# Split f32r projections for five more xbc tiles, a held SSD decay and a new stage order in a one-core S5/SSD/retention trunk

## Chip, cores and metric

The kernel runs on 1 core of one Trainium2 chip. The metric is device time in microseconds, the median of the runs. The engines are named as in the profile: PE or TensorE (matmuls), ACT (ScalarE), DVE (VectorE), POOL (GpSimd) and SP (SyncE, which issues all DMAs here).

## What is computed

Input x is (1, 512, 1024) in float32; the trunk has two layers and a final RMSNorm. Layer 0, in which the change lies, is this, cut to what matters:

```python
p = rmsnorm(h) @ w_in                     # 1024 -> z 2048 | S5 input 1024 | xBC 1536 | dt 16
y_a = s5_mixer(p[S5 input], ...) * silu(z[:1024])
xbc = silu(causal_depthwise_conv(p[xBC], conv_w, conv_b))     # 4 taps
dt  = softplus(p[dt] + dt_bias)
a_cs = cumsum(dt * a)                                         # in chunks of 128 steps
y_diag = (C B^T * exp(segsum(a_cs))) @ (xs * dt)              # decay matrix per head
states, y_off = chunk states, C @ previous state * exp(a_cs)
y_b = rmsnorm((y_diag + y_off + xs * D) * silu(z[1024:]), groups=2)
h = h + concat([y_a, y_b]) @ w_out
```

S5 is a diagonal complex recurrence; its gated output passes a GLU. Layer 1 is a four-head retention layer, untouched by the change.

## The kernel before

All activations lie transposed, features on the 128 partitions and the 512 steps along the free axis, so 1024 features are 8 tiles x0 to x7. Each output tile of 128 columns of the input projection is one "projection": 8 matmuls over the 8 input tiles into one PSUM bank (tag acc, 3 banks).

There are two forms of a projection (`proj`, L214). Plain (`mm1`, L210): 8 float32 matmuls of the raw weight with the normed input xn. Split (`mm3`, L111): weight and input are each the sum of a part rounded to f32r and a remainder, and 24 f32r matmuls make high x high, high x low and low x high. The weight is split after its load by `split_w` (L101): ACT rounds it (L107), DVE subtracts (L108), both with the rank of `rank_w`. Names in the list `SPLIT` (L29) take the split form. The input's parts xh and xl are made by stage `w` (`parts`, L259, through `split`, L119). The 16 parts and xn0 to xn6 share the 16 buffers of tag "x", so seven parts take over a buffer of xn and wait until all plain projections that are traced before have read it. Plain weights use seven buffers (tags raw, wh, wl in turn); split ones have three raw buffers and two each for the two parts.

The work of layer 0 is cut into stages, which `ORDER` (L36) lists by letter and number: d and e make dt and its cumulative sums (e also writes a_cs to DRAM), x is a projection of xBC with its convolution (`conv`, L345), u one of the S5 input, z one of the gate (written to DRAM, L432), s an SSD chunk's setup (`ssd`, L359) and t its output (`ssd_y`, L409), w the input's parts, n and r the SSD norm (root and use), o a tile of the output projection's SSD half (`out_b`), p a tile of the S5 gate (`glu_in`). S5 has q (parameters and the rotation table on POOL), l, g, a (load, state products and scan of a group), b and k (kernel and taps), c (its output).

A scheduler turns this into one queue for each engine: it runs a list of instructions against a simulated timeline and, of those that are ready, takes the one with the lowest priority number, which by default counts up in the order of tracing. `rank_w` gives weight splits -2000000 and `rank_e` (L92) gives evacuations of PSUM -1000000, plus a count. A queue is then fixed, and each engine takes its instructions in that order.

Stage x: ACT evacuates the bank with the last tap and the bias (L349), DVE adds the other three taps from PSUM (L352, rank_e), ACT applies SiLU (L354). The bank is free after the last tap. Stage s transposes the chunk's x into PSUM (tag b, 3 banks); DVE evacuates it twice, with dt (xdt, L380) and with the decay to the chunk's end (xds, L384); PE makes the chunk's state (L387) and the part of the previous state (L390), which DVE evacuates into yos (L392); DVE moves the running state on (L406, L407). For the decay matrix, a_cs is loaded as a broadcast (512 KB, L395), ACT takes 8 absolute differences (L397) and one exponential (L398), DVE multiplies by C B^T (L399).

At the start, u0 and u1 are projected from the scaled, not yet normed x (L247, L249). The squares are added on DVE (L243), `root` (L162) sums them over partitions with matmuls into rs0ps and takes the inverse square root in small DVE steps (L150 to L159), `spread` (L172) transposes it into rs0pb, ACT copies it (L176), and DVE makes xn (L251).

Of the kernel before, what the change touches and what calls it, by code (L numbers as in the profile page):

```python
# [14 lines left out]
AF = mybir.ActivationFunctionType  # L15
ALU = mybir.AluOpType
# [9 lines left out]
BUFS = {'x': 16, 'v': 17, 'm': 20, 's': 4, 'p': 5, 'f': 8}  # L26
POOL_P = ((1, 1), (2, 1), (3, 1))
WARM = 11
SPLIT = [f"z{m}" for m in range(16)] + [f"u{m}" for m in range(2, 8)]  # L29
SILU_Z = tuple(range(8, 16))  # L30
GELU_P = ()
AX, AZ = 200, 600
KEEP = (2, 3)
POOL_Z = (7,)
VEC_X = ((0, 0), (1, 0), (0, 1), (1, 1))
ORDER = """d0 x8 x10 x9 e0 x11 q0 x0 b0 x1 x2 l0 g0 x3 x4 k0 x5 b1 x6 a0 x7 w0 g1 s0 u2 u3 l1 t0 s1 z0 a1 k1 b2 z1 t1 s2 u4 c0 u5  # L36
 t2 l2 g2 s3 z2 a2 k2 b3 z3 t3 u6 c1 u7 z4 l3 g3 z5 n0 z6 a3 z7 c2 n1 z8 k3 r0 z9 r1 z10 c3 z11 o0 p0 p1 o1 z12 p2 z13 p3 o2 z14
 p4 p5 z15 o3 p6 p7 o4 o5 o6 o7"""
MAGIC = 12582912.0
LOG2E = 1.4426950408889634  # L40
LN2_HI = 0.693359375
# [7 lines left out]
def trunk_kernel(ctx: ExitStack, tc: tile.TileContext, a: dict, out: bass.AP):  # L49
# [98 lines left out]
    def rsqrt_small(y, ss, n, name, w=4):  # L148
# [6 lines left out]
        for it in range(3):  # L155
# [3 lines left out]
            vec.scalar_tensor_tensor(y, t, 1.5, cur, op0=ALU.add, op1=ALU.mult)  # L159
            cur = y  # L160

    def root(sqs, n, name):  # L162
        ps = aux(name + "ps")
        for c in range(NC4):
            for i, s in enumerate(sqs):
                pe.matmul(ps[:, c:c + 1], s[:, c * P:(c + 1) * P], ones,
                          start=i == 0, stop=i == len(sqs) - 1)
        y = sm.tile([P, 4], F32, name=name + "y", tag="rs_y", bufs=4)
        rsqrt_small(y, ps[:, 0:4], n, name)
        return y  # L170

    def spread(y, name, bc):  # L172
        pb = aux(name + "pb")
        for c in range(NC4):
            pe.transpose(pb[:, c * P:(c + 1) * P], y[:, c:c + 1].broadcast_to([P, P]), ident)
        act.activation(bc, pb, AF.Copy)  # L176

    def rstd(sqs, n, name, bc):
        y = root(sqs, n, name)
        spread(y, name, bc)  # L180
        return y
# [12 lines left out]
    def layer0():  # L194
# [33 lines left out]
        with rank(-3000000):  # L228
            s5pr = t("m", "s5p", n=192).rearrange("p (i w) -> p i w", w=64)
            sp.dma_start(s5pr, a["s5p"])  # L230
            sp.dma_start(lnw, a["lnw"])
            w0 = []
            for k in range(KD):
                sp.dma_start(xs[k], a["xT"][k])
                if k == 0:
                    w0 += [ld_raw(a["w_u"][m], f"u{m}") for m in range(1)]
            w0 += [ld_raw(a["w_u"][m], f"u{m}") for m in range(1, 2)]
            for k in range(KD):
                q = t("p", f"xq{k}")
                act.activation(q, xs[k], AF.Square)  # L240
                act.activation(xs[k], xs[k], AF.Identity, scale=lnw[:, 0, k:k + 1])
                if k:
                    vec.tensor_tensor(sq[0], sq[0], q, op=ALU.add)  # L243
                sq.append(q)
            pu = [acc(f"u{m}") for m in range(2)]
            for k in range(KD):
                pe.matmul(pu[0], w0[0][:, k, :], xs[k], start=k == 0, stop=k == KD - 1)  # L247
            rstd(sq[:1], D, "rs0", rbc)
            mm1(pu[1], w0[1], xs)  # L249
            for k in range(KD):  # L250
                vec.tensor_tensor(xn[k], xs[k], rbc, op=ALU.mult)  # L251
        tri = const("tri", [P, P], a["tri"])
# [88 lines left out]
            sp.dma_start(at_d.rearrange("c h l -> h c l"), aT)  # L341

        xbc = [None] * 12

        def conv(m):  # L345
            ps = proj(a["w_xbc"][m], f"xbc{m}", ahead=AX)
            g = t("v", f"cva{m}")
            with rank_e():
                act.activation(g, ps, AF.Identity, scale=cvw[:, m, 3:4], bias=cvw[:, m, 4:5])  # L349
                for j in range(2, -1, -1):  # L350
                    d = 3 - j
                    vec.scalar_tensor_tensor(g[:, d:], ps[:, 0:SEQ - d], cvw[:, m, j:j + 1], g[:, d:],  # L352
                                             op0=ALU.mult, op1=ALU.add)
            act.activation(g, g, AF.Silu)  # L354
            xbc[m] = g
        prev = [None, None]
        held = {}

        def ssd(c):  # L359
            yb, bT, cT = xbc[0:8], xbc[8:10], xbc[10:12]  # L360
# [13 lines left out]
            for gr in range(2):  # L374
                hs = slice(8 * gr, 8 * gr + 8)
                xdt = t("v", f"xdt{c}{gr}").rearrange("p (h d) -> p h d", d=64)
                ps_x = aux(f"px{c}{gr}", "b")
                for i in range(4):
                    pe.transpose(ps_x[:, i * P:(i + 1) * P], xbc[4 * gr + i][:, cs], ident)
                vec.tensor_tensor(xdt, ps_x.rearrange("p (h d) -> p h d", d=64),  # L380
                                  dtn[:, c, hs].unsqueeze(2).broadcast_to([P, 8, 64]), op=ALU.mult)
                if c < NC4 - 1:
                    xds = t("v", f"xds{c}{gr}")
                    vec.tensor_tensor(xds.rearrange("p (h d) -> p h d", d=64), ps_x.rearrange("p (h d) -> p h d", d=64),  # L384
                                      ds[:, c, hs].unsqueeze(2).broadcast_to([P, 8, 64]), op=ALU.mult)
                    ps_s = aux(f"st{c}{gr}", "b")
                    pe.matmul(ps_s, bn[:, gr, :], xds, start=True, stop=True)  # L387
                if c > 0:
                    ps_o = aux(f"yo{c}{gr}", "b")
                    pe.matmul(ps_o, cT[gr][:, cs], prev[gr], start=True, stop=True)  # L390
                    yo = t("v", f"yos{c}{gr}")
                    vec.tensor_tensor(yo.rearrange("p (h d) -> p h d", d=64), ps_o.rearrange("p (h d) -> p h d", d=64),  # L392
                                      ec[:, c, hs].unsqueeze(2).broadcast_to([P, 8, 64]), op=ALU.mult)
                dec = tp.tile([P, 8, P], F32, name=f"dec{c}{gr}", tag="g", bufs=3)
                sp.dma_start(dec, at_d[c, hs, :].partition_broadcast(P))  # L395
                for i in range(8):
                    act.activation(dec[:, i, :], dec[:, i, :], AF.Abs, bias=nacs[:, c, 8 * gr + i:8 * gr + i + 1])  # L397
                act.activation(dec, dec, AF.Exp, scale=-1.0)  # L398
                vec.tensor_tensor(dec, dec, cbm[:, gr, :].unsqueeze(1).broadcast_to([P, 8, P]), op=ALU.mult)  # L399
                held[c, gr] = xdt, dec, yo if c > 0 else None  # L400
                if c == 0:
                    prev[gr] = t("s", f"prev{gr}")
                    act.activation(prev[gr], ps_s, AF.Copy)
                elif c < NC4 - 1:
                    h_ = prev[gr].rearrange("p (h d) -> p h d", d=64)
                    vec.tensor_tensor(h_, h_, cd[:, c, hs].unsqueeze(2).broadcast_to([P, 8, 64]), op=ALU.mult)  # L406
                    vec.tensor_tensor(prev[gr], prev[gr], ps_s, op=ALU.add)  # L407

        def ssd_y(c):  # L409
            yb, cs = xbc[0:8], slice(c * P, (c + 1) * P)  # L410
# [731 lines left out]
```

## Time and profile before

| what | value |
|---|---|
| three runs | 917.1, 919.69 (median), 923.75 us |
| the profiled execution | 923.73 us |
| its span, first to last instruction | 921.9 us |
| mean granted clock of TensorE | 0.970 |
| busy: PE, DVE, ACT, POOL | 881.6, 524.6, 360.3, 212.7 us |

The profile shows one execution. Times in rows are microseconds from the span's start unless marked ns; a name such as xbc4w is a tile of the program, L212 a line of the code. A busy PE is not PE at its peak, since the ends of matmuls are modelled. "Granted clock" is the share of TensorE's full clock that the chip let it have in a stretch; 1.00 is 2.4 GHz.

### The profile page before, as it was taken

What the parts mean: (1) busy time and instruction counts of PE and PEld (TensorE: products, weight loads), DVE (VectorE), ACT (ScalarE), POOL (GpSimd) and SP (SyncE); (2) the same over time, 40 slices, a digit from 0 to 9 for tenths busy, and PEclk for the clock granted to TensorE, in tenths of its full rate; (3) what the DMA queues carried; (4) which work ended last, traced back from release to release, by engine and by line L of the source; (5) the groups of instructions that cost most, each with busy time, mean ns of one, the idle gap of its engine ahead of it and who ended that gap; (6) DMA issues with size and microseconds to landing.
All of it is one profiled execution on the core that took longest, in us unless ns stands there. A gap on an engine that the chain in (4) does not pass through costs nothing.

```text
span 921.9 us, 11425 instructions
## 1 busy us (share of the span) xinstructions
PE 881.6 (96%) x4308; PEld 678.6 (74%) x4308; DVE 524.6 (57%) x917; ACT 360.3 (39%) x571; POOL 212.7 (23%) x187
## 2 busy tenths in 40 slices
PE   8899797989989999999999999999999999999996
PEld 4244355757768877788888888888888888888885
DVE  6967469784873365443454463744743644547445
ACT  4344632515216444523344225345421244254432
POOL 0059983070472500000003121301000303110020
PEclk9999899979999888999999999999999999999999
DMA  7377142666549636573543222222222221222322
GB/s 242 113 211 249 50 128 69 187 201 180 146 130 311 216 132 190 182 245 125 202 141 103 92 91 69 74 86 69 92 92 94 93 90 66 92 69 69 114 69 92
DMA packets 64184, 121.45 MB, mean 132 GB/s; under 512 B 18112, under 2 KB 28672, under 8 KB 64000
## 3 DMA queue, kind: packets, MB, share of 16 engines
q1 hardware_dynamic: 64128, 120.71, 40.7%
q8 instruction: 34, 0.56, 0.3%
q14 instruction: 22, 0.18, 0.1%
HBM read 103.61 MB, written 17.07 MB: 131 GB/s over the span
## 4 chain that ended last, share of the span: by engine, by line
PE 76%; DVE 11%; issue 4%; ACT 4%; DMA 2%; POOL 1%; SPq 0%; DVEq 0%; POOLq 0%; ACTq 0%
PE xbc L212 3%; PE qk L117 3%; PE g L115 3%; PE qk L116 3%; PE g L116 3%; PE g L117 3%; PE qk L115 3%; PE v L921 3%; PE v L922 3%; PE v L920 3%; PE z L117 2%; PE z L115 2%; PE z L116 2%; PE ob L116 2%; PE ob L117 2%
## 5 line engine op out<-in xcount | busy, mean ns | idle before, releaser
L894 POOL TENSOR_TENSOR rt<-rt,ru 128x512 f32<-128x512 f32 x16 | 27.2, 1721 | 134.6 <-DVE ru L893 134.6
L963 POOL TENSOR_TENSOR os<-os,os 128x512 f32<-128x512 f32 x12 | 15.5, 1290 | 139.8 <-ACT os L961 106.9
L352 DVE SCALAR_TENSOR_TENSOR cva<-xbc,cvw,cva 128x511 f32<-128x511 f32 (+2 forms) x36 | 26.8, 743 | 25.8 <-ACT cva L349 25.4
L789 POOL TENSOR_TENSOR O<-ct,s5pws 128x512 f32<-128x512 f32 x16 | 23.1, 1441 | 50.0 <-DVE prev L407 42.0
L873 POOL TENSOR_TENSOR hs<-hs,hs 128x512 f32<-128x512 f32 x7 | 12.2, 1749 | 92.4 <-ACT hs L871 92.4
L397 ACT ACTIVATE dec<-dec,nacs 128x128 f32<-128x128 f32 x64 | 19.4, 389 | 33.6 <-DMA dec<-at_d 33.6
L893 DVE TENSOR_TENSOR ru<-qk,tab 128x512 f32<-128x512 f32 x16 | 10.9, 684 | 32.5 <-PE qk L117 32.5
L793 POOL TENSOR_TENSOR O<-O,ot 128x512 f32<-128x512 f32 x16 | 24.6, 1563 | 0.0
L452 POOL TENSOR_TENSOR za6r<-za6r,y 128x512 f32<-128x512 f32 x1 | 2.2, 2247 | 86.3 <-DMA h_d<-hb 86.3
L789 POOL TENSOR_TENSOR ot<-ct,s5pws 128x512 f32<-128x512 f32 x16 | 21.7, 1355 | 0.0
L733 POOL TENSOR_TENSOR tm<-al,b 128x512 f32<-128x512 f32 x6 | 8.1, 1371 | 55.6 <-DMA b<-in_s5bP_dram 32.9
L995 DVE TENSOR_TENSOR h<-h,out 128x512 f32<-128x512 f32 x8 | 5.5, 686 | 25.5 <-PE out L117 25.5
L1056 POOL TENSOR_TENSOR fin<-fin,fnw 128x512 f32<-128x512 f32 x4 | 5.0, 1289 | 59.5 <-ACT fq L1020 59.5
L836 PE MATMUL Y<-T,U 128*64 128x128 f32 x128 | 18.4, 311 | 0.0
L526 POOL TENSOR_TENSOR s5rt<-rot,s5lv 128x512 f32<-128x512 f32 (+4 forms) x7 | 5.9, 837 | 52.8 <-DVE s5lv L668 52.8
L490 DVE TENSOR_TENSOR hb<-ob,hb 128x512 f32<-128x512 f32 x8 | 5.5, 690 | 20.9 <-PE ob L117 20.8
L416 PE MATMUL y<-ident,yos 128*128 128x128 f32 x48 | 12.6, 349 | 4.6 <-DVE yos L392 4.6
L839 ACT ACTIVATE ysb<-Y 128x256 f32<-128x256 f32 x16 | 5.2, 380 | 29.9 <-PE Y L836 18.8
L733 DVE TENSOR_TENSOR tm<-al,b 128x512 f32<-128x512 f32 x10 | 11.3, 1168 | 9.9 <-DMA b<-in_s5bP_dram 6.8
L519 DVE TENSOR_TENSOR h<-oa,h 128x512 f32<-128x512 f32 x8 | 5.5, 691 | 19.6 <-PE oa L117 19.6
L835 PE MATMUL Y<-Or,X 128*64 128x128 f32 x64 | 14.5, 314 | 1.5 <-DMA Or<-o_d 1.5
L120 ACT ACTIVATE rh<-rt 128x512 fp32r<-128x512 f32 (+1 forms) x16 | 9.1, 577 | 16.9 <-POOL rt L894 16.9
(1697 smaller groups left out, 2972.3 us busy)
## 6 DMA issues: line engine op xcount, KB each, us to landing
al<-al_d SPq DMA_DIRECT2D x8, 512.0 KB
b<-in_s5bP_dram SPq DMA_DIRECT2D x8, 512.0 KB
dec<-at_d SPq DMA_DIRECT2D x8, 512.0 KB
o_d<-O SPq DMA_DIRECT2D x16, 256.0 KB
T<-kd SPq DMA_DIRECT2D x64, 64.0 KB
Or<-o_d SPq DMA_DIRECT2D x16, 256.0 KB
x<-in_xT_dram SPq DMA_DIRECT2D x8, 256.0 KB
u_d<-us SPq DMA_DIRECT2D x8, 256.0 KB
```

The source lines that it names most:

```text
L115: pe.matmul(ps, wh[:, k, :], xh[k], start=start and i == 0, stop=False)
L116: pe.matmul(ps, wh[:, k, :], xl[k], start=False, stop=False)
L117: pe.matmul(ps, wl[:, k, :], xh[k], start=False, stop=stop and i == len(ks) - 1)
L212: pe.matmul(ps, raw[:, k, :], x[k], start=k == 0, stop=k == KD - 1)
L352: vec.scalar_tensor_tensor(g[:, d:], ps[:, 0:SEQ - d], cvw[:, m, j:j + 1], g[:, d:], op0=ALU.mult, op1=ALU.add)
L397: act.activation(dec[:, i, :], dec[:, i, :], AF.Abs, bias=nacs[:, c, 8 * gr + i:8 * gr + i + 1])
L789: pool.tensor_tensor(x.rearrange("p (g k c) -> p g k c", g=4, c=16), ct[:, c, par, 4 * hf:4 * hf + 4].unsqueeze(2).broadcast_to(sh), pws[: ...
L793: pool.tensor_tensor(o, o, tm, op=ALU.add)
L894: pool.tensor_tensor(t1, t1, t2, op=op)
L920: pe.matmul(ps[c], hh[kk][:, cs], wh[:, i, :], start=kk == 0, stop=False)
L921: pe.matmul(ps[c], hh[kk][:, cs], wl[:, i, :], start=False, stop=False)
L922: pe.matmul(ps[c], hl[kk][:, cs], wh[:, i, :], start=False, stop=kk == KD - 1)
```

## The change

Five xbc projections (m = 3 to 7) take the split form. Stage w stands behind x2 instead of behind x7, and x3 to x6 follow each other. A few z tiles, the glu_in and the out_b tiles change places. At the start u1's matmuls are queued on PE behind the root's. ACT's absolute differences of the decay are queued behind the last evacuation of a conv stage that was traced before them, which is xbc7's for all chunks. Six DVE steps of the SSD setup get the rank of evacuations.

```diff
-SPLIT = [f"z{m}" for m in range(16)] + [f"u{m}" for m in range(2, 8)]
+SPLIT = [f"z{m}" for m in range(16)] + [f"u{m}" for m in range(2, 8)] + [f"xbc{m}" for m in range(3, 8)]
...
-ORDER = """d0 x8 x10 x9 e0 x11 q0 x0 b0 x1 x2 l0 g0 x3 x4 k0 x5 b1 x6 a0 x7 w0 g1 s0 u2 u3 l1 t0 s1 z0 a1 k1 b2 z1 t1 s2 u4 c0 u5
- t2 l2 g2 s3 z2 a2 k2 b3 z3 t3 u6 c1 u7 z4 l3 g3 z5 n0 z6 a3 z7 c2 n1 z8 k3 r0 z9 r1 z10 c3 z11 o0 p0 p1 o1 z12 p2 z13 p3 o2 z14
- p4 p5 z15 o3 p6 p7 o4 o5 o6 o7"""
+ORDER = """d0 x8 x10 x9 e0 x11 q0 x0 b0 x1 x2 w0 l0 g0 x3 x4 x5 x6 k0 b1 a0 x7 g1 s0 u2 u3 l1 t0 s1 z0 a1 z1 k1 b2 t1 s2 u4 c0 u5
+ t2 l2 g2 s3 z2 a2 z3 k2 b3 t3 u6 c1 u7 z4 l3 g3 z5 n0 z6 a3 z7 c2 n1 z8 k3 r0 z9 z10 r1 c3 z11 p0 p1 z12 p2 z13 p3 o0 o1 z14
+ p4 p5 o2 z15 p6 p7 o3 o4 o5 o6 o7"""
...
+    held0 = [None]
+
     def root(sqs, n, name):
...
-                pe.matmul(ps[:, c:c + 1], s[:, c * P:(c + 1) * P], ones,
-                          start=i == 0, stop=i == len(sqs) - 1)
+                held0[0] = pe.matmul(ps[:, c:c + 1], s[:, c * P:(c + 1) * P], ones,
+                                     start=i == 0, stop=i == len(sqs) - 1).ins
...
-            rstd(sq[:1], D, "rs0", rbc)
-            mm1(pu[1], w0[1], xs)
+            y0, last = root(sq[:1], D, "rs0"), held0[0]
+            with tc.issue_after(last):
+                mm1(pu[1], w0[1], xs)
+            spread(y0, "rs0", rbc)
...
-                act.activation(g, ps, AF.Identity, scale=cvw[:, m, 3:4], bias=cvw[:, m, 4:5])
+                held["conv"] = act.activation(g, ps, AF.Identity, scale=cvw[:, m, 3:4], bias=cvw[:, m, 4:5]).ins
...
-                vec.tensor_tensor(xdt, ps_x.rearrange("p (h d) -> p h d", d=64),
-                                  dtn[:, c, hs].unsqueeze(2).broadcast_to([P, 8, 64]), op=ALU.mult)
+                with rank_e():
+                    vec.tensor_tensor(xdt, ps_x.rearrange("p (h d) -> p h d", d=64),
+                                      dtn[:, c, hs].unsqueeze(2).broadcast_to([P, 8, 64]), op=ALU.mult)
...
-                for i in range(8):
-                    act.activation(dec[:, i, :], dec[:, i, :], AF.Abs, bias=nacs[:, c, 8 * gr + i:8 * gr + i + 1])
+                with tc.issue_after(held["conv"]):
+                    for i in range(8):
+                        act.activation(dec[:, i, :], dec[:, i, :], AF.Abs, bias=nacs[:, c, 8 * gr + i:8 * gr + i + 1])
```

The steps of xds, yos and the running state (two) are put under rank_e in the same way as xdt. `issue_after(ins)` puts an edge of order, without a semaphore, from `ins` to each instruction in the block on the same engine.

## Rows read from the trace of the kernel before

**Rows 1.** Page, part 2: TensorE's busy tenths and granted clock, 40 slices.
```profile
PE   8899797989989999999999999999999999999996
...
PEclk9999899979999888999999999999999999999999
```

**Rows 2.** TensorE's waits, 20 to 440 us: us in total, times, longest.
```profile
PE xbc L212 <- issue: 6.2, 2, 5.1
PE y L416 <- DVE yos L392: 4.6, 1, 4.6
PE u L117 <- DVE u3l L108: 3.7, 1, 3.7
...
PE ob L115 <- ACT ybh L120: 2.2, 1, 2.2
```

**Rows 3.** Windows: length, busy PE, PEld, DVE, ACT, POOL, PEclk, DMA share, GB/s.
```profile
86.00:126.00 40.00, 34.94 (x111) 15.35 (x110) 13.92 (x22) 22.53 (x39) 38.45 (x44) 0.91 0.24 92
126.00:198.00 72.00, 62.53 (x405) 46.07 (x403) 65.77 (x87) 23.18 (x43) 27.00 (x18) 0.96 0.50 152
...
198.00:210.00 12.00, 12.00 (x80) 8.50 (x80) 5.53 (x13) 4.70 (x14) 7.10 (x6) 0.55 0.59 199
335.00:350.00 15.00, 12.46 (x85) 10.35 (x84) 8.80 (x24) 7.72 (x12) 0.00 (x0) 0.61 0.41 124
```

**Rows 4.** Timeline of TensorE, 80 to 137: start, length, instruction [idle before, releaser].
```profile
81.27 7.11 PE L212 MATMUL xbc<-xn,xbc2w 128*128 128x512 f32 x16 [1.11 <-issue]
88.21 7.03 PE L212 MATMUL xbc<-xn,xbc3w 128*128 128x512 f32 x16
...
100.64 9.93 PE L212 MATMUL xbc<-xn,xbc4w 128*128 128x512 f32 x16 [5.06 <-issue]
...
136.14 0.61 PE L364 MATMUL cb<-cva,cva 128*128 128x128 f32 x4
```

**Rows 5.** Timeline of TensorE, first matmuls of two split projections.
```profile
179.78 0.50 PE L115 MATMUL u<-xh,u4h 128*128 128x512 f32 x1
...
185.36 0.39 PE L115 MATMUL u<-xh,u5h 128*128 128x512 f32 x1
```

**Rows 6.** Timelines of ACT, DVE and POOL around u2's weight split and the table's end.
```profile
110.61 1.06 ACT L107 ACTIVATE u2h<-u2w 128x1024 fp32r<-128x1024 f32 x1 [0.59 <-PE xbc L212]
...
111.70 1.23 DVE L108 TENSOR_TENSOR u2l<-u2w,u2h 128x1024 fp32r<-128x1024 f32 x1 [2.40 <-ACT u2h L107]
...
110.69 1.06 POOL L525 TENSOR_TENSOR s5rt<-rot,s5lv 128x512 f32<-128x512 f32 x1
111.71 2.13 POOL L526 TENSOR_TENSOR s5rt<-rot,s5lv 128x512 f32<-128x512 f32 x1
...
131.45 1.28 POOL L530 TENSOR_TENSOR rot<-s5rt 128x512 f32<-128x512 f32 x1
```

**Rows 7.** Timeline of ACT: decay steps, and the idle time behind xbc7's evacuation.
```profile
83.74 4.77 ACT L397 ACTIVATE dec<-dec,nacs 128x128 f32<-128x128 f32 x16
...
152.58 0.60 ACT L403 ACTIVATE prev<-st 128x512 f32<-128x512 f32 x1 [13.62 <-PE st L387]
```

**Rows 8.** Timeline of DVE, 45 to 210: xbc1's taps.
```profile
98.22 2.32 DVE L352 SCALAR_TENSOR_TENSOR cva<-xbc,cvw,cva 128x511 f32<-128x511 f32 x3 [11.01 <-ACT cva L349]
```

**Rows 9.** Timelines of ACT and TensorE at the start.
```profile
13.25 1.93 ACT L241 ACTIVATE x<-x,lnw 128x512 f32<-128x512 f32 x3
...
19.33 0.95 PE L166 MATMUL rs0ps<-ones,xq 128*128 128x1 f32 x8
...
25.66 0.62 PE L175 MATMUL rs0pb<-ident,rs0y 128*128 128x128 f32 x4 [1.84 <-DVE rs0y L159]
```

**Rows 10.** Timelines of DVE and TensorE around yos.
```profile
193.16 2.01 DVE L108 TENSOR_TENSOR z2l<-z2w,z2h 128x1024 fp32r<-128x1024 f32 x1
...
196.71 0.69 DVE L392 TENSOR_TENSOR yos<-yo,dcd 128x512 f32<-128x512 f32 x1
...
197.45 0.80 PE L416 MATMUL y<-ident,yos 128*128 128x128 f32 x2 [4.55 <-DVE yos L392]
```

More of the change, by code (lines that the diff above doesn't have):

```diff
@@ L343, in layer0 @@
         xbc = [None] * 12
+        held = {}
         def conv(m):
@@ L356, in layer0 @@
         prev = [None, None]
-        held = {}
         def ssd(c):
@@ L379, in ssd @@
                     pe.transpose(ps_x[:, i * P:(i + 1) * P], xbc[4 * gr + i][:, cs], ident)
-                vec.tensor_tensor(xdt, ps_x.rearrange("p (h d) -> p h d", d=64),
-                                  dtn[:, c, hs].unsqueeze(2).broadcast_to([P, 8, 64]), op=ALU.mult)
+                with rank_e():
+                    vec.tensor_tensor(xdt, ps_x.rearrange("p (h d) -> p h d", d=64),
+                                      dtn[:, c, hs].unsqueeze(2).broadcast_to([P, 8, 64]), op=ALU.mult)
                 if c < NC4 - 1:
                     xds = t("v", f"xds{c}{gr}")
-                    vec.tensor_tensor(xds.rearrange("p (h d) -> p h d", d=64), ps_x.rearrange("p (h d) -> p h d", d=64),
-                                      ds[:, c, hs].unsqueeze(2).broadcast_to([P, 8, 64]), op=ALU.mult)
+                    with rank_e():
+                        vec.tensor_tensor(xds.rearrange("p (h d) -> p h d", d=64), ps_x.rearrange("p (h d) -> p h d", d=64),
+                                          ds[:, c, hs].unsqueeze(2).broadcast_to([P, 8, 64]), op=ALU.mult)
                     ps_s = aux(f"st{c}{gr}", "b")
@@ L391, in ssd @@
                     yo = t("v", f"yos{c}{gr}")
-                    vec.tensor_tensor(yo.rearrange("p (h d) -> p h d", d=64), ps_o.rearrange("p (h d) -> p h d", d=64),
-                                      ec[:, c, hs].unsqueeze(2).broadcast_to([P, 8, 64]), op=ALU.mult)
+                    with rank_e():
+                        vec.tensor_tensor(yo.rearrange("p (h d) -> p h d", d=64), ps_o.rearrange("p (h d) -> p h d", d=64),
+                                          ec[:, c, hs].unsqueeze(2).broadcast_to([P, 8, 64]), op=ALU.mult)
                 dec = tp.tile([P, 8, P], F32, name=f"dec{c}{gr}", tag="g", bufs=3)
                 sp.dma_start(dec, at_d[c, hs, :].partition_broadcast(P))
-                for i in range(8):
-                    act.activation(dec[:, i, :], dec[:, i, :], AF.Abs, bias=nacs[:, c, 8 * gr + i:8 * gr + i + 1])
+                with tc.issue_after(held["conv"]):
+                    for i in range(8):
+                        act.activation(dec[:, i, :], dec[:, i, :], AF.Abs, bias=nacs[:, c, 8 * gr + i:8 * gr + i + 1])
                 act.activation(dec, dec, AF.Exp, scale=-1.0)
@@ L405, in ssd @@
                     h_ = prev[gr].rearrange("p (h d) -> p h d", d=64)
-                    vec.tensor_tensor(h_, h_, cd[:, c, hs].unsqueeze(2).broadcast_to([P, 8, 64]), op=ALU.mult)
-                    vec.tensor_tensor(prev[gr], prev[gr], ps_s, op=ALU.add)
+                    with rank_e():
+                        vec.tensor_tensor(h_, h_, cd[:, c, hs].unsqueeze(2).broadcast_to([P, 8, 64]), op=ALU.mult)
+                        vec.tensor_tensor(prev[gr], prev[gr], ps_s, op=ALU.add)
         def ssd_y(c):
```

## The prediction

> **What bounds the kernel now.** I read the page's slices first: from the 17th on TensorE and its granted clock stand at 9 tenths in every slice but the last, so I take what layer 0 gains to pass through to the end; the larger holes, and the slices with a lower granted clock, lie in the first 16, some 369 us [rows 1]. Next I read TensorE's waits there: the three longest are one of xbc (5.1), one of y for yos (4.6) and one of u3 for its weight remainder (3.7) [rows 2]. Then the windows around these holes, for the other engines and the clock: granted 0.55 in 198 to 210, after the wait for yos, and 0.61 in 335 to 350 around the wait of ob, a mixture of the two levels 1.2 and 2.4 GHz [rows 3]. A hole thus costs more than its idle time. Last I read the queues of ACT and DVE at each hole, to see what stood in front of the instruction that was late.
>
> **The change part by part.** The sum is made against the profiled execution, 923.73 us around a span of 921.9; the median of the three runs is 919.69, that is 4.0 lower, and I take this off at the end.
>
> *Five projections split.* An unsplit projection of 8 matmuls shows as 16 passes and takes 6.94 us from start to start (xbc2 at 81.27, xbc3 at 88.21) [rows 4]. A split one is 24 f32r matmuls and takes 5.58 (u4 at 179.78, u5 at 185.36) [rows 5]. Five times 1.36 is **-6.8**. For each, the split adds one ACT rounding of the weight (1.06) and one DVE subtraction (1.23) [rows 6]. In 86 to 126 ACT is busy for 22.5 of 40 us and DVE for 13.9 [rows 3], so 5.3 and 6.2 us more find room there; without that cover each late remainder stops TensorE as u3's did. The weights are loaded as before, 512 KB each; what changes is that they use three buffers and no longer seven.
>
> *The remainders' cost elsewhere.* While u2's subtraction ran at 111.70, a GpSimd product took 2.13 where the one before it, of the same shape, took 1.06 [rows 6]. Five more subtractions can thus put back GpSimd's last write of the rotation table, which ends at 132.73, by 5 x 1.07 = 5.4. The Trainium skill (SBUF — State Buffer, section Who interferes with whom) states that these two engines share one port pair as an exclusive lock, and that the loser is blocked for the whole instruction; by it the five would cost GpSimd 5 x 1.23 = 6.2. The trace agrees, with 1.07 of 1.23 for one. The term runs from 0 (all hidden) to +7.4 (two waits like u3's 3.7 [rows 2]); I take one of these, **+3.7**, the nearest row for a late remainder.
>
> *Decay held until the last conv tap.* xbc4's matmuls need the PSUM buffer of xbc1, whose taps on DVE waited 11.01 us for ACT's evacuation and ran from 98.22 to 100.54 [rows 8]; xbc4 starts at 100.64 after 5.06 of standing, which the view puts down to issue [rows 4]. In front of the evacuation ACT had run decay steps, 16 in one go from 83.74 on and 8 more, with their exponentials and table loads [rows 7]. xbc4 then takes 9.93 where xbc2 takes 7.11 [rows 4]: 2.8 more at the lower clock. With the decay steps behind xbc7's evacuation, xbc1's can start at 83.7, and with xbc0's and its own taps (2.3 each) its buffer is free at about 88.5, where xbc4 will ask for it at 88.2 + 5.6 at the earliest. Both parts go, **-7.9**. Nothing on ACT is late next: the held steps (24 x 0.30 = 7.2) and three exponentials like the weight rounding (1.06) come to some 12 us with a table load, and ACT stood idle for 13.62 before 152.58, behind xbc7's evacuation [rows 7]. Without that cover the decay is late for the first y by as much as doesn't fit, some us. Ends: -7.9 and, if another buffer holds xbc4 as long, 0.
>
> *Input parts earlier.* Seven of the 16 parts take over the buffers of xn0 to xn6 and so wait for the last plain projection, now xbc2 where it was xbc7. Their roundings and subtractions trail xbc2's matmuls, and xbc3 needs them only after half of its own. If the queues are free it costs 0; if the last subtractions stand behind two sets of taps (2.3 each [rows 8]) it costs 5. The taps of xbc0 and xbc1 are just then due; I take **+1.5**, nearer to 0, since xbc3's first half covers 2.8 of it.
>
> *Root before the second u.* The root's matmuls stand at 19.33, behind most of u1; now all of u1 follows them. The last input scaling ends at 15.2, the six last passes of u0 (6.94 / 16 = 0.43 each), which need it, at 16.5, and the root's matmuls (0.95) at 17.4. The DVE chain behind them (5.4, from 20.3 to 25.66) ends at 22.8, and u1's 6.9 cover it until 24.3. The spread starts then and not at 25.66 [rows 9]: **-1.4**. If it is put inside u1, it starts 2.8 earlier, the lower end; if TensorE waits out the last three scalings (1.93), it is +1.9.
>
> *SSD evacuations preferred.* TensorE stood for 4.55 before 197.45 for yos; DVE came to it at 196.71, after z2's remainder at 193.16 (2.01) and a scan addition that ended then [rows 10], and then the clock of 0.55 over 12 us lost 5.4 more [rows 3]. With the new rank the scan's additions fall behind yos; z2's remainder has the higher rank and may stay. From 0 (something else at the head) to -10; I take **-5**, the idle time and little of the clock.
>
> *z tiles moved.* ob0 waited 2.2 for ybh [rows 2], and the clock of 0.61 over 15 us lost 5.9 [rows 3]. Now z11, z12 and z13 lie between the norm's last step and the first out_b tile, and glu_in's steps and DMAs come earlier in their queues. From -8.1 to +2.2 (one such wait anew); I take **-3**.
>
> Sum: -6.8 + 3.7 - 7.9 + 1.5 - 1.4 - 5.0 - 3.0 = -18.9. 923.7 less 18.9 is 904.8, less 4.0 is 900.8: **901** beside the median of 919.69.
>
> **Rivals.**
> *DVE swallows the first stage's gain.* In 126 to 198 DVE is busy for 65.8 of 72 us [rows 3]. The 13.2 us that TensorE gains before the first SSD step (6.8 + 7.9 - 1.5) are worth what DVE can start earlier, and the scan of group 0 can't: it needs the rotation table of 132.73. For it: two of the three longest waits name DVE. Against it: DVE is idle for 26 us in 86 to 126, and the SSD steps and weight remainders can use them. With half of 13.2 kept, -1.4 for the start, nothing from yos and -1 from z it gives -9.0: 910.7.
>
> *The rotation table stops split xbc7 (the slower side).* Before, xbc7 needed nothing from DVE. Now its remainder stands in DVE's queue, and the scan of group 0 is put in front of xbc7 in the stage list. If the scan's products stand ahead of that remainder, xbc7 waits for the table: 132.7 + 5.4 = 138.1, then three products and the remainder (some 3.2 together), xbc7 (5.6) and the 2.8 that xbc4 lost by the clock end at 149.7, where the first SSD matmul (cb) started at 136.14 [rows 4]. That is +13.6; yos, in the same queue, gains nothing, z gives -3: +10.6, 930.3. With that order it is slower from a table that ends after 127.5 on, which the trace has now. For it: GpSimd is busy for 38.5 of 40 us in 86 to 126 [rows 3]. Against it: weight remainders have the highest rank, so they stand behind the scan only if the order was made with a table expected much earlier.
>
> *All clocks recover.* With the lower ends -2.8, -10 and -8.1 and no cost added: -35.6, 884.1. For it: each low clock followed a hole that the change aims at. Against it: DVE and GpSimd have no more time than before.
>
> That the hold of the decay does nothing is no case of weight: the edge is to xbc7's evacuation, after which no conv is traced.
>
> **How the numbers follow.** The forecast has 0.60, the swallowed gain 0.18, all clocks 0.12, the table's stop 0.10. A measurement tells about 1% from no change, 9.2 us: below 910.5 is faster, above 928.9 slower. The swallowed case falls on both sides of 910.5, and a little of the forecast lies above it: faster 0.78, same 0.13, slower 0.09. The range reaches from near all clocks to past the swallowed case, 886 to 918.
>
> **What would show it.** Right: xbc3 to xbc7 start some 5.6 apart with no wait of 5 us; the first cb starts near 123 and not at 136.14; no decay step on ACT before xbc7's evacuation; the wait of y for yos under 2; a clock of 0.9 or more around the first ob. Wrong: xbc7 or u2 waiting several us for a remainder while DVE stands at the scan's first products, a new wait of xbc3 for its input parts, or a first-stage gain that is gone by 200.

## The result and the profile after

The kernel after takes 912.38 us (median of 7 runs, 909.22 to 915.33), the kernel before on the same chip 921.75 (7 runs): a ratio of 0.9881, 95% interval 0.9856 to 0.9906. (The ratios here are those on record; the quotient of the two medians is 0.9898. Figures in us that are worked out from two ratios are estimates.) It is 9.4 us faster where 18.9 were forecast. The time lies inside the range, which was made to reach past the case of the first rival; it lies above the 910.5 below which the prediction saw 0.78 of the chances. The profiled execution took 915.33 us, 8.4 less than that of before and 2.95 above its kernel's median, with a mean granted clock of 0.975.

The page's slices of after, TensorE and its granted clock, answer to [rows 1]:

```profile
PE   8999955989989899999999999999999999999996
...
PEclk9999977979999899999999999999999999999999
```

The holes of the early slices are gone, and a new one stands in the sixth and seventh, 114 to 160 us, with a clock of 7 tenths. TensorE's waits of after, 20 to 440 us (in total, times, longest), say for what, as [rows 2] did:

```profile
PE z L117 <- DVE z0l L108: 7.8, 1, 7.8
PE u L115 <- DVE cva L357: 5.2, 1, 5.2
PE u L117 <- DVE u3l L108: 4.2, 1, 4.2
PE y L425 <- DVE yos L399: 3.8, 1, 3.8
```

The waits of xbc for issue and of ob for ybh don't appear any more. The first three lines are new or longer, and all three name DVE (yos L399 is yos L392 of before). Windows of after (length, busy PE, PEld, DVE, ACT, POOL, then clock, DMA share, GB/s), beside [rows 3]:

```profile
86.00:126.00 40.00, 38.45 (x240) 30.78 (x238) 25.82 (x31) 12.66 (x19) 38.22 (x39) 1.00 0.29 94
124.00:161.00 37.00, 17.74 (x57) 12.56 (x56) 35.98 (x37) 19.98 (x40) 30.71 (x19) 0.72 0.32 100
340.00:360.00 20.00, 19.02 (x116) 14.71 (x109) 14.08 (x28) 9.78 (x17) 0.00 (x0) 0.93 0.58 157
```

and the middle one of the kernel before:

```profile
124.00:161.00 37.00, 32.08 (x166) 22.25 (x165) 34.55 (x43) 9.87 (x15) 18.45 (x13) 0.95 0.36 113
```

In 86 to 126 TensorE now stands for 1.6 us and not 5.1, at full clock. In 124 to 161 it is busy for half the time, while DVE is full and GpSimd has 30.7 us of work where it had 18.5. TensorE's timeline of after (start, length, instruction), to lay beside [rows 4, 5]:

```profile
83.55 0.79 PE L115 MATMUL xbc<-xh,xbc3h 128*128 128x512 f32 x1
...
117.95 0.38 PE L368 MATMUL cb<-cva,cva 128*128 128x128 f32 x2
...
161.07 0.39 PE L115 MATMUL z<-xh,z1h 128*128 128x512 f32 x1
...
177.30 0.39 PE L115 MATMUL u<-xh,u4h 128*128 128x512 f32 x1
```

From xbc3 to the first cb it takes 34.4 us where before took 47.93. The starts of such marks in the kernels' profiled executions, in us (f2, g5 and g8 are experiments, below):

| mark | before | after | f2 | g5 | g8 |
|---|---|---|---|---|---|
| dt | 28.03 | 26.47 | 26.73 | 26.93 | 27.67 |
| xbc3 | 88.21 | 83.55 | 83.80 | 84.01 | 87.85 |
| first cb behind xbc7 | 136.14 | 117.95 | 118.22 | 118.43 | 134.94 |
| u3 | 141.59 | 129.70 | 129.99 | 128.75 | 146.18 |
| z1 | 157.16 | 161.07 | 155.49 | 153.94 | 162.34 |
| u4 | 179.78 | 177.30 | 171.72 | 170.16 | 167.94 |
| z2 | 214.19 | 212.31 | 203.54 | 196.31 | 207.82 |
| z10 | 320.35 | 317.81 | 305.16 | 285.10 | 310.97 |
| z15 | 388.68 | 380.80 | 368.35 | 370.26 | 385.04 |
| first tile of layer 0's GLU | 422.77 | 414.29 | 401.43 | 403.04 | 417.81 |

After is 18.2 us ahead at the first cb, 2.5 at u4, 2.5 at z10, 7.9 at z15 and 8.5 at the GLU. (In after, f2 and g5 two of the four matmuls of the first cb ran early, at 76.9 to 77.3; the mark is the one behind xbc7. z1, u4 and z2, and z10 in g5, stand elsewhere among the other matmuls in some lists, so they compare only kernels with one list; before and after have nearly the same matmuls ahead of u4 and of z10.) So the first stage gains what was forecast and more, 15.7 of it is gone at u4, nothing is won in the SSD steps, and the tail brings 5.4.

DVE's queue of after in that stretch shows what u3 and z0 waited for:

```profile
120.78 0.68 DVE L767 TENSOR_TENSOR gi<-S,rot 128x504 f32<-128x504 f32 x1 [4.21 <-POOL rot L536]
124.31 0.68 DVE L768 TENSOR_TENSOR X<-S,rot 128x504 f32<-128x504 f32 x1 [2.85 <-POOL rot L539]
...
128.82 0.73 DVE L357 SCALAR_TENSOR_TENSOR cva<-xbc,cvw,cva 128x509 f32<-128x509 f32 x1
...
133.49 1.52 DVE L108 TENSOR_TENSOR u3l<-u3w,u3h 128x1024 fp32r<-128x1024 f32 x1
...
137.10 3.81 DVE L772 TENSOR_TENSOR_SCAN X<-mg,gi 128x512 f32<-128x512 f32 x2
...
141.47 2.75 DVE L775 TENSOR_TENSOR gi<-X,rot 128x512 f32<-128x512 f32 x2
144.15 0.73 DVE L357 SCALAR_TENSOR_TENSOR cva<-xbc,cvw,cva 128x509 f32<-128x509 f32 x1
...
145.83 2.28 DVE L407 TENSOR_TENSOR dec<-dec,cbn 128x1024 f32<-128x1024 f32 x1
...
151.49 2.17 DVE L108 TENSOR_TENSOR z0l<-z0w,z0h 128x1024 fp32r<-128x1024 f32 x1
...
156.07 1.23 DVE L407 TENSOR_TENSOR dec<-dec,cbn 128x1024 f32<-128x1024 f32 x1
```

Two things are to be seen. DVE stands for 7.06 us for the rotation table, with the last tap of xbc7 (128.82), which frees the buffer u3 needs, and u3's remainder queued behind. And from there on it works almost without a gap, but some of its instructions take longer than alone: dec's product 2.28 at 145.83 and 1.23 at 156.07, z0's remainder 2.17 where such a one takes 1.23. GpSimd's queue of after over the same time:

```profile
122.98 1.30 POOL L539 TENSOR_TENSOR rot<-s5rt 128x512 f32<-128x512 f32 x1
124.24 1.10 POOL L798 TENSOR_TENSOR O<-ct,s5pws 128x512 f32<-128x512 f32 x1
...
143.65 3.38 POOL L802 TENSOR_TENSOR O<-O,ot 128x512 f32<-128x512 f32 x2
146.99 2.25 POOL L745 TENSOR_TENSOR al<-al,b 128x512 f32<-128x512 f32 x1
...
150.87 1.71 POOL L745 TENSOR_TENSOR al<-al,b 128x512 f32<-128x512 f32 x1
```

and that of before, where the same products of stage b1 stand:

```profile
115.15 1.10 POOL L789 TENSOR_TENSOR O<-ct,s5pws 128x512 f32<-128x512 f32 x1
...
125.64 5.85 POOL L793 TENSOR_TENSOR O<-O,ot 128x512 f32<-128x512 f32 x4
```

Before, b1 ran from 115.15 to 131.49, ahead of the table's last write and mostly beside a DVE with little to do. After, the table ends 8.45 us earlier (124.28 for 132.73 [rows 6]) and b1 runs behind it, beside the scan of group 0, up to 147.03. The products of group 1 (tm and al, L742 to L746) stand mixed with it and behind it in GpSimd's queue and end at 154.79; z0's remainder at 151.49 runs beside these. Of each DVE instruction that starts in 124 to 161 I took its length less the shortest of its line and shape in the same trace: this excess, as it is called below, sums to 7.2 us before and 12.0 after, and in 180 to 200 to 4.4 before and 8.8 after.

DVE's two marks around the scan in the kernel before are

```profile
148.34 2.32 DVE L763 TENSOR_TENSOR_SCAN X<-mg,gi 128x512 f32<-128x512 f32 x2
...
156.56 1.21 DVE L108 TENSOR_TENSOR z0l<-z0w,z0h 128x1024 fp32r<-128x1024 f32 x1
```

From the scan's first instruction to the end of z0's remainder DVE has eleven instructions in both kernels. Their shortest lengths sum to 10.1 us before and 9.7 after; their excess is 0.05 before and 7.4 after.

### The profile page after: what moved, and what is told of

Same layout as the page of the kernel before. It is cut to its first block, busy times and chain, and to the rows that moved or that the text cites. A ratio compares the mean times of both kernels' runs of the same rounds, so it can differ in the third digit from the quotient of the medians.

```text
span 913.6 us, 11520 instructions
## 1 busy us (share of the span) xinstructions
PE 868.6 (95%) x4348; PEld 683.1 (75%) x4348; DVE 542.5 (59%) x922; ACT 359.5 (39%) x572; POOL 229.3 (25%) x187
## 4 chain that ended last, share of the span: by engine, by line
PE 68%; DVE 12%; POOL 8%; DMA 5%; SPq 2%; issue 2%; ACT 1%; ACTq 0%; POOLq 0%; DVEq 0%
PE g L115 3%; PE qk L117 3%; PE qk L116 3%; PE g L117 3%; PE g L116 3%; PE qk L115 3%; PE v L930 3%; PE v L931 3%; PE v L929 3%; PE gl L116 2%; PE gl L117 2%; PE gl L115 2%; PE out L117 2%; PE oa L116 2%; PE oa L117 2%
## 5 line engine op out<-in xcount | busy, mean ns | idle before, releaser
L798 POOL TENSOR_TENSOR ot<-ct,s5pws 128x512 f32<-128x512 f32 x16 | 28.1, 1756 | 0.0
L802 POOL TENSOR_TENSOR O<-O,ot 128x512 f32<-128x512 f32 x16 | 27.3, 1736 | 0.0
L742 POOL TENSOR_TENSOR tm<-al,b 128x512 f32<-128x512 f32 x6 | 9.0, 1513 | 57.3 <-DMA b<-in_s5bP_dram 34.2
L359 ACT ACTIVATE cva<-cva 128x512 f32<-128x512 f32 x12 | 7.6, 631 | 33.7 <-DVE cva L357 33.6
```

What stands on the lines that cost most here:

```text
L798: pool.tensor_tensor(x.rearrange("p (g k c) -> p g k c", g=4, c=16), ct[:, c, par, 4 * hf:4 * hf + 4].unsqueeze(2).broadcast_to(sh), pws[: ...
L802: pool.tensor_tensor(o, o, tm, op=ALU.add)
```

## The experiments

The theory at the outset was that DVE, in one queue with the table's wait at its head, gives the first stage's gain back; the rival was that parts of the change add up but are smaller than forecast.

**e2_hold_only**: the kernel before with the decay hold alone.

```diff
-                for i in range(8):
-                    act.activation(dec[:, i, :], dec[:, i, :], AF.Abs, bias=nacs[:, c, 8 * gr + i:8 * gr + i + 1])
+                with tc.issue_after(held["conv"]):
+                    for i in range(8):
+                        act.activation(dec[:, i, :], dec[:, i, :], AF.Abs, bias=nacs[:, c, 8 * gr + i:8 * gr + i + 1])
```

> The kernel before with the decay hold alone. The hold's own theory (xbc1's evacuation no longer behind 24 decay steps): the 5.06 us wait of xbc4 and the 2.8 us it loses to the clock go, so the first cb starts some 8 us earlier than 136.14. The theory that the stage behind (rotation table ending near 132, DVE busy 65.8 of 72 us) swallows what is gained before it: cb earlier, but u4 within 2 us of before's 179.78 and the total within 0.5% of before (ratio 0.995 to 1.003). If instead the gain passes through, the ratio is near 0.991.

925.81 us, ratio 1.0026 (0.9999 to 1.0053). Its waits:

```profile
PE Y L836 <- DMA Or<-o_d: 11.7, 4, 7.8
PE st L387 <- DVE xds L384: 5.7, 2, 3.6
...
PE xbc L212 <- issue: 1.3, 1, 1.3
```

The 5.06 of xbc4 are gone, and from xbc3 to the first cb it takes 39.48 us, 8.45 less than before (forecast 7.9). u5 starts at 198.44, 13 us later than before, and nothing is left at the end. Of the waits that are new or longer, two name DVE (st's, and one of 4.6 of u for xl), but the largest is Y's for a load by DMA, 11.7 where it was 2.5; so this run doesn't show DVE alone as what takes the gain.

**e3_old_tail**: the kernel after with the stage list of before from s0 on (z11 to z14, out_b and glu_in in their old places, and z1, z3 and z10 too, which the cut list here doesn't show).

```diff
- ... r0 z9 z10 r1 c3 z11 p0 p1 z12 p2 z13 p3 o0 o1 z14 p4 p5 o2 z15 p6 p7 o3 ...
+ ... r0 z9 r1 z10 c3 z11 o0 p0 p1 o1 z12 p2 z13 p3 o2 z14 p4 p5 z15 o3 p6 p7 ...
```

> The changed kernel with the stage list of before from s0 on (z, glu_in and out_b tiles in their old places). Theory: the lasting part of the gain is the moved tail, since the changed trace is only 1.9 to 3.3 us ahead of before from u5 to z10 and 8 ahead at z15. Then this kernel keeps about 2.5 to 3 us: ratio 0.996 to 0.999. Rival (the lasting gain comes from the first stage): ratio stays near 0.988 to 0.990.

917.12 us, 0.9939 (0.9916 to 0.9963). Up to z5 it follows the kernel after (277.61 for 276.26), waits of DVE and all. The moved z, out_b and glu_in tiles are thus worth 0.0058, some 5.3 us, and all the rest of the change 0.0061.

**e4_table_early** and **e6_a0_late**: the kernel after with the table's neighbours moved (b0 behind x4, k0 behind x7), and with the scan of group 0 (a0) behind u3.

```diff
- ... q0 x0 b0 x1 x2 w0 l0 g0 x3 x4 x5 x6 k0 b1 a0 x7 ... u2 u3 l1
+ ... q0 x0 x1 x2 w0 l0 g0 x3 x4 b0 x5 x6 b1 a0 x7 k0 ... u2 u3 l1
+ ... q0 x0 b0 x1 x2 w0 l0 g0 x3 x4 x5 x6 k0 b1 x7 ... u2 u3 a0 l1
```

> The changed kernel with b0 (16 us of POOL products and 5 of sums) moved from behind x0 to behind x4, and k0 behind x7, so that POOL can finish the rotation table before it. Theory A (the DVE queue stands still for the table: 4.21 + 2.85 us, with weight remainders behind it): the table ends some 15 us or more earlier than 124.3, those two waits vanish, the waits of u3 (5.2 and 4.2) shrink to under 3 together, u4 starts 5 us or more earlier than 177.3, ratio 0.980 to 0.984. Theory B (DVE has too much work there, doubled in length by POOL's share of the port): the waits move to other remainders and the total stays within 2 us of the changed kernel, ratio 0.986 to 0.990.

> The changed kernel with a0, the scan of group 0, behind u3 instead of between x6 and x7. Theory A (scan products that wait for the table stand in DVE's queue before u3's remainder and xbc7's taps): without them in front the u3 waits of 5.2 and 4.2 go, z0 starts near 130 where it started at 145, but the scan's work then comes later; total 3 to 6 us better than the changed kernel, ratio 0.982 to 0.985. Theory B (DVE's total work bounds the stage): waits move to z0, z1 and yos, total within 2 us, ratio 0.986 to 0.990.

912.45 us, 0.9889 (0.9851 to 0.9928), and 911.62 us, 0.9895 (0.9831 to 0.9959): both as the kernel after. The first missed its purpose, since GpSimd's new order ended the table at 148.09 and not earlier. It moved b1 as well, out of the stretch and ahead of the table's last blocks (GpSimd's timeline):

```profile
101.44 6.02 POOL L802 TENSOR_TENSOR O<-O,ot 128x512 f32<-128x512 f32 x4
...
146.81 1.28 POOL L539 TENSOR_TENSOR rot<-s5rt 128x512 f32<-128x512 f32 x1
```

The excess of 124 to 161 fell to 2.7 us with it. A table 23.8 us later and a collision that is gone may thus have cancelled, and the run doesn't show that the table's end is free. In the second u3 waited 11.7 for xbc7's taps, which still stood behind the table. Neither tells what the wait for the table costs by itself.

**f1_table_short**: the kernel after with the table's last block copied by ACT.

```diff
+                if k0 == 16:
+                    act.activation(yr, xr, AF.Copy)
+                    act.activation(yi, xi, AF.Copy)
+                    continue
```

> The kernel after, with the last of the seven blocks of the rotation table copied by ACT and not multiplied on GpSimd (the second half of its last doubling; the table's last 16 columns thus hold other values). GpSimd's last product and the table then end some 7 us earlier, near 117. Theory A (the gain of the first stage is lost while DVE stands 4.21 and 2.85 us for the table): z1 and u4 start 5 to 7 us earlier than in the kernel after and the gain lasts, ratio to the kernel before 0.980 to 0.983. Theory B (it is lost because DVE and GpSimd together have too much work between 124 and 200, their instructions side by side longer than alone): GpSimd has 7 us less to do there too, so some 4 to 7 us stay, 0.981 to 0.984. Theory C (a later regulator takes whatever the first stage gains): 0.986 to 0.990, as the kernel after.

917.05 us, 0.9949 (0.9926 to 0.9972). The copy itself spoiled the first stage: it stands at the head of ACT's queue and waits there for GpSimd, with xbc6's rounding behind it, for which TensorE then waits 7.3 us (ACT's timeline):

```profile
105.68 0.63 ACT L691 ACTIVATE rot<-rot 128x512 f32<-128x512 f32 x1 [11.83 <-POOL rot L536]
```

So its total says nothing of the theories. Its middle does say something: GpSimd's table ended at 117.02, the first cb came at 129.48, and z0 still waited 7.8 for its remainder. z1 is at 162.34, as late as in the kernel after, whose first cb was 11.5 us earlier. With no wait of the scan for the table (its first products run at 126.53 without one), DVE's work beside b1 (here 126.96 to 148.92) and the products behind it kept z0's remainder back as long.

**f2_b1_short**: the kernel after with eight of b1's twelve GpSimd instructions left out.

```diff
-                for c, x in enumerate((o, tm)):
+                for c, x in enumerate((o,) if j == 1 else (o, tm)):
...
-                pool.tensor_tensor(o, o, tm, op=ALU.add)
+                if j != 1:
+                    pool.tensor_tensor(o, o, tm, op=ALU.add)
```

> The kernel after, with the second product and the sum of b1 left out (b1's four tiles hold one product each): eight of the twelve GpSimd instructions of b1 go, some 13 us of GpSimd between 124 and 147, beside which DVE's instructions of 124 to 161 took 11.8 us more than the shortest of their shapes. The table stays where it is. Theory A (only the table's wait matters): 0.986 to 0.990, as the kernel after, DVE standing for the table as before. Theory B (GpSimd's work beside DVE matters): u4 starts 5 us or more earlier and it lasts, 0.980 to 0.984. Theory C (a later regulator): u4 earlier, but 0.986 to 0.990.

903.15 us, 0.9799 (0.9762 to 0.9836). DVE's queue in it is that of after but for single steps, with the wait for the table in its place:

```profile
124.60 0.68 DVE L768 TENSOR_TENSOR X<-S,rot 128x504 f32<-128x504 f32 x1 [2.18 <-POOL rot L539]
...
142.45 1.28 DVE L775 TENSOR_TENSOR gi<-X,rot 128x512 f32<-128x512 f32 x2
...
144.91 1.21 DVE L407 TENSOR_TENSOR dec<-dec,cbn 128x1024 f32<-128x1024 f32 x1
...
147.47 1.23 DVE L108 TENSOR_TENSOR z0l<-z0w,z0h 128x1024 fp32r<-128x1024 f32 x1
```

The instructions of 2.75, 2.28 and 2.17 take 1.28, 1.21 and 1.23, z0's remainder comes 4.0 us earlier, z1 and u4 5.6, and it lasts: 0.0082 less than after, some 7.6 us. The excess of the eleven instructions falls from 7.4 to 1.5. With the wait for the table in its place (7.05 us), this tells the collision from it and from a later regulator. GpSimd's products of group 1, which stand behind b1, end at 140.80 here and not at 154.79, and are a part of what no longer collides.

**e1_split_only**: the kernel before with the split and the new list up to x7, without hold, root and preference.

> The kernel before with the five projections split and the stage list of the kernel after up to x7, the old list from s0 on; no decay hold, no early root, no preferred evacuations. If the parts of the change add up as forecast: first cb near 129, 6.8 less 3.7 us faster, ratio 0.996 to 0.997. If the split and the hold each gain in the first stage but DVE and GpSimd give it back: first cb 4 to 9 us earlier than before, u5 not earlier, 0.998 to 1.006. If the split's arithmetic is the whole of what lasts of the first stage: 0.992 to 0.994.

919.96 us, 0.9974 (0.9951 to 0.9996). Waits in its first stage:

```profile
PE xbc L115 <- ACT xh L120: 4.1, 1, 4.1
PE xbc L212 <- issue: 3.5, 1, 3.5
```

From xbc3 to the first cb it takes 45.21 us, 2.7 less than before, with the hold alone 8.45 less, with both (after) 13.5 less. Counted from dt, which takes in the wait of 3.5 before xbc2, the split alone is 2.5 us slower up to there (110.6 for 108.1), the hold alone 9.8 faster and after 16.6. ACT's decay steps delay the parts of the input too, and the split pays only when they are out of the way.

**e7_no_rank**: the kernel after without the preference for the SSD evacuations.

> The kernel after without the preference for the six SSD evacuations. If the preference is worth the 5 us that were forecast: the wait of y for yos is 4 us or more longer than the 3.8 of the kernel after, ratio 0.992 to 0.995. If DVE's other work stands in front of yos anyway: wait of 3 to 6 us, ratio 0.986 to 0.990.

914.17 us, 0.9911 (0.9876 to 0.9945). The interval overlaps that of after, so what the preference is worth stays open, but not 5 us for yos: y waits for it 1.8 us without and 3.8 with it (and cb for the running state 1.8 without and 0.2 with it), and it stands ahead of z2's remainder either way (192.35 and 195.53 here).

**g2_b12_gate** and **g3_b123_gate**: the kernel after with all of b's work, moved. The edit shown is that of g2; g3 has b3 behind z6 as well, with its load behind that of z6's weights, and k3 behind z9.

```diff
+        with ExitStack() as es:
+            if j in {1: 'u5', 2: 'u7'}:
+                es.enter_context(after({1: 'u5', 2: 'u7'}[j]))
+            sp.dma_start(ct, a["s5c"][j])
- ... x6 k0 b1 a0 ... z1 k1 b2 t1 s2 u4 c0 u5 t2 l2 g2 s3 z2 a2 z3 k2 b3 t3 u6 c1 u7 z4 ...
+ ... x6 k0 a0 ... z1 t1 s2 u4 c0 u5 b1 t2 l2 g2 s3 z2 k1 a2 z3 b3 t3 u6 c1 u7 b2 z4 k2 ...
```

> The kernel after with the whole work of b1 and b2 kept, but moved: b1 stands behind u5 and b2 behind u7 in the stage list, their first load behind the loads of u5's and u7's weights (issued at 153.7 and 199.9), k1 behind z2 and k2 behind z4. GpSimd's products then run beside the stretches in which DVE is busy for 15.8 and 11 of 20 us, and not beside 124 to 161. If the collision beside the scan of group 0 takes the gain: DVE's scan instructions there near the shortest of their shapes, z0l some 4 us and z1 5 us earlier than in the kernel after, and it lasts, ratio 0.979 to 0.984. If the products only collide elsewhere for as long: z1 earlier, gl0 not, 0.986 to 0.990. If the outputs of group 1 or 2 come late (Y waiting for Or or T by 4 us and more): 0.988 to 0.995.

> As the kernel with b1 and b2 moved, and b3 behind z6, its first load behind that of z6's weights (243.6), k3 behind z9: GpSimd's products of group 3 then run from some 250 on in part beside an idle DVE and not beside the scan of group 2 (249 to 268), whose instructions took up to 1.7 times the shortest. If the collision is what costs: some 2 to 4 us less than with b1 and b2 alone. If TensorE is covered there (it was busy for 20 of 20 us in 240 to 260): the same within 2 us. If group 3 comes late for c3: slower than that by 3 us or more.

909.24 us, 0.9838 (0.9810 to 0.9866), and 909.36 us, 0.9850 (0.9823 to 0.9877). The excess of 124 to 161 falls from 12.0 to 3.7 and 3.5 us, that of 180 to 200 from 8.8 to 0.6 and 0.5, and z1 starts 7.5 us earlier in g2; it is 16.4 us ahead of after at z2. But b3 and b2 now run beside the scan of group 2 and behind it, and of that lead 1.8 us are left at the GLU (412.54). Its longest wait is new:

```profile
PE z L117 <- DVE z7l L108: 6.2, 1, 6.2
```

Moving b3 as well brought nothing that can be told from this.

**g5_b_spread**: as g2, with b2 right behind b1 and k1, without a gate of its own, and b3 behind z6, its load behind that of z6's weights.

```diff
+ ... u5 b1 t2 l2 g2 s3 z2 k1 b2 a2 z3 t3 u6 k2 c1 u7 z4 l3 g3 z5 n0 z6 b3 a3 z7 c2 n1 z8 k3 ...
```

> The kernel after with GpSimd's products of the three later groups spread over the stretches in which DVE is light: b1 behind u5 (gated by the load of u5's weights, as in the kernel with b1 and b2 moved), b2 behind b1 and k1, b3 behind z6 and gated by the load of z6's weights. In the kernel with b1 and b2 moved, b3's products ran from 236.7 to 256 beside the scan of group 2 and b2's from 273.8 on, and of 16 us gained at z2 some 4 were left at the end. If the collisions with the scans are what gives the gain back each time: z2 near 196, z8 below 285, ratio 0.974 to 0.980. If the work only finds another place in which DVE is late: 0.981 to 0.986, with the gain of z2 gone by gl0 as before.

903.68 us, 0.9801 (0.9765 to 0.9837), on the edge between the two bands (z2 at 196.31 and z8 at 274.00 are as the first has them), and the best version with all the work in it: 0.0080 below the kernel after, some 7.4 us. The excess of the eleven instructions is 1.5 here too. DVE's queue shows the short lengths again, behind the same wait for the table:

```profile
124.78 0.68 DVE L768 TENSOR_TENSOR X<-S,rot 128x504 f32<-128x504 f32 x1 [2.85 <-POOL rot L539]
...
140.91 1.28 DVE L775 TENSOR_TENSOR gi<-X,rot 128x512 f32<-128x512 f32 x2
...
143.37 1.21 DVE L407 TENSOR_TENSOR dec<-dec,cbn 128x1024 f32<-128x1024 f32 x1
```

and TensorE's waits and its window of 124 to 161 show what is left:

```profile
PE Y L847 <- DMA Or<-o_d: 5.5, 2, 5.1
PE u L117 <- DVE u3l L108: 4.9, 1, 4.9
PE u L115 <- DVE cva L357: 3.8, 1, 3.8
PE z L117 <- DVE z0l L108: 3.0, 1, 3.0
...
PE y L425 <- DVE yos L399: 0.5, 1, 0.5
```

```profile
124.00:161.00 37.00, 25.35 (x119) 18.57 (x118) 32.96 (x49) 21.00 (x42) 11.36 (x7) 0.82 0.43 125
```

z0's wait falls from 7.8 to 3.0 and that for yos from 3.8 to 0.5. u3's two waits stay, since its buffer and its remainder still stand behind the table. The longest wait is now one of Y for a DMA (5.1, where the longest of after was 1.5).

**g8_before_spread**: the kernel before with the spread of g5.

> The kernel before (plain projections, no hold) with the same spread of b1, b2 and b3. There b1's products ran from 115 to 131, beside an idle DVE and ahead of the last piece of the rotation table. Theory (the change gained 18 us up to the first SSD step and lost them because b1 came to stand beside the scan): without the first stage's gain the spread has the table some 7 us earlier to offer and little else, ratio 0.990 to 0.998, and the kernel after with the spread is faster than this one by 10 us or more. Rival (the spread is a gain of its own, and the first stage's is lost whatever GpSimd does): 0.980 to 0.988, and the two kernels with the spread are within 5 us of one another.

917.18 us, 0.9947 (0.9924 to 0.9970). The spread alone is worth 0.5% to the kernel before, so not all of g5's 0.0080 is owed to b1's new place in after. The kernel after with it is 13.5 us (0.0146) faster than this one, where without the spread the two differ by 9.4 (0.0119). That fits a gain of which b1's place took part, but the difference of the two is inside their intervals; what b1 costs in after rests on f2 and g2.

## Why the prediction was right or wrong

*Direction, and where it would show.* Right: no wait of xbc of 5 us, xbc3 to xbc6 some 5.4 to 6.3 apart (xbc7 9.2 behind xbc6, with other matmuls between), the first cb at 117.95 where 123 was named, no decay step on ACT before xbc7's evacuation, the granted clock 0.93 in 340 to 360 around the first ob. The wait of y for yos under 2 didn't come. Of the signs against it one came: of the first stage's 18.2 us 2.5 are left at u4. Another came in a near form: not xbc7 or u2 but u3 waited, 5.2 and 4.2 us, behind the scan's first products. So a time inside the range was in part luck: the terms up to the first cb hold, but the path behind it was not the one forecast, and the range was wide enough for both.

*Five projections split and decay held* (-6.8 and -7.9, with +1.5 for the input's parts: -13.2). Measured from xbc3 to the first cb: -13.5. The sum is right. What the prediction didn't see is that the parts need one another (-2.7 and -8.45 alone, or +2.5 and -9.8 from dt). The +1.5 for the input's parts doesn't show in after: xbc3 has no wait.

*Root before the second u* (-1.4). Measured -1.56 at the start of dt (28.03, 26.47). In both executions the last input scalings start alike, 13.25 [rows 9] and 13.26, so the first loads took no part in it; the spread starts at 24.46, where 24.3 was worked out:

```profile
13.26 1.93 ACT L243 ACTIVATE x<-x,lnw 128x512 f32<-128x512 f32 x3
...
24.46 0.60 PE L177 MATMUL rs0pb<-ident,rs0y 128*128 128x128 f32 x4
```

Between dt and xbc3 another 3.1 went, unforeseen: 1.1 is the wait before xbc2, and most of the rest the clock, granted at 0.91 in 28 to 45 before, behind two waits of 1.8 and 1.7, and at 1.00 in the same stretch of after, behind one of 1.4. The term had left the clock out.

*The remainders' cost elsewhere* (+3.7, at most +7.4). This is the step that failed: 15.7 us were given back between the first cb and u4. The term priced the remainders' share of DVE and the delay they give the table. The table came earlier, and what the prediction had no term for is stages k0 and b1 put behind x6 in the list, past the end of the table: b1's first load went from 95.66 to 105.64, and its products from 115.15 to 124.24, beside DVE's scan.

The queues show where the lead goes. It is 18.2 us at the first cb and 11.2 where DVE's scan starts (148.34, 137.10): some 7.0 are lost while DVE stands 7.06 for the table. It is 4.1 where z0's remainder ends: another 7.1 are lost over the eleven instructions with their excess of 7.4. It is 1.9 at z0's last matmul: TensorE, which had stood 7.8 for that remainder, took 7.5 us for z0's last 22 matmuls at a granted clock of 0.68, a mixture of the two levels, where before took 5.3 at 1.00:

```profile
157.80:163.10 5.30, 5.30 (x24) 4.39 (x24) 5.17 (x7) 0.18 (x1) 0.00 (x0) 1.00 0.83 237
153.70:161.20 7.50, 7.48 (x23) 5.98 (x24) 6.66 (x7) 0.15 (x1) 1.09 (x1) 0.68 0.61 166
```

(the first line is before, the second after). The second part of the loss is shown by experiment: f2 gains 5.6 us at u4 with two thirds of b1's instructions gone, g2 7.5 at z1 with all of them moved. The first is read from the queues alone: what the wait for the table costs by itself wasn't separated, since f1 made a new wait and e4 moved b1 with the table; in g5 u3 still waits 8.7 us behind it.

*SSD evacuations preferred* (-5). Measured none: y still waits 3.8 for yos. The prediction saw z2's remainder and a scan addition ahead of it, and put the additions behind yos by the new rank. The remainder stands behind yos now (197.70 and 194.35), without the rank too (e7), but three of the scan's additions are still ahead of it and run beside b2's products (excess of 8.8 in 180 to 200). Where b1 and b2 are moved (g5) the wait is 0.5.

*z tiles moved* (-3). Measured -5.4 from z10 to z15 and 0.0058 by e3; the wait of ob for ybh (2.2) is gone and the clock recovers (0.70 to 0.93 in 340 to 360). Mis-sized: more of the clock came back than I took.

*The rivals.* "DVE swallows the first stage's gain" (910.7) was nearest in time and in place. Its reason, a scan that can't start before the table, is good for some 7 us of the loss as the queues read, which no run shows by itself; DVE and GpSimd working side by side, which it did not name, for as much again. Its sum also took half the gain for lost without a row that says half. "The rotation table stops split xbc7" fell: xbc7's remainder was no issue, and the table ended earlier. That g5 is 18.4 us faster than the kernel before, nearly the 18.9 of the forecast, doesn't make the forecast right: g5 moves b1, b2 and b3 as well.

## What to carry to other kernels

When a list of stages is reordered, lay out what each engine's queue does beside every other one's, and not only beside TensorE: a block of GpSimd work that moved by 9 us, from beside an idle DVE to beside a full one, took back 5.6 to 7.5 of an 18 us gain, and a queue that stood for a table some 7 more. Put GpSimd's work where DVE has little to do, and look for DVE instructions that take longer than the same shape elsewhere in the trace. Two edits can each be worth little alone (split, hold) and more together, so a term for one should say which of the others it needs.

## What was unexpected about the hardware

GpSimd beside it stretches only some of DVE's instructions. In after, products of two SBUF tiles were stretched (dec 2.28 for 1.23, z0's remainder 2.17 for 1.23), and in 180 to 200 too. Those with one operand in PSUM were not: the taps take 0.73 at 144.15, in the midst of b1, the first scan products (from PSUM and the table) 0.66 to 0.68 in every kernel, and in all fourteen traces none that reads the banks of xbc, S, cb, px, yo or st between 100 and 220 us is more than 0.04 above the shortest of its line and shape. The Trainium skill (SBUF — State Buffer, section Who interferes with whom) states that a DVE instruction with two SBUF inputs contends with a GpSimd one that reads SBUF, and that outside the 2-port modes one with a single SBUF input does not; its section SBUF: two separate sides adds that whichever starts first has the port pair for the whole instruction and the other is blocked. The traces agree on the first two. On the third one place can be followed: dec starts at 145.83 beside b1's last sum, which ends at 147.03, and ends at 148.11, 1.08 later, of 1.22 alone; GpSimd's next product, al at 146.99, ends 1.13 behind dec, of 1.27 alone. Each needs about its own length once the other has ended, as that sentence would have it.
